# A recurrent layer's chunk chain: state and u in one tile, outputs directly behind their operands, v centred by a matmul, a third buffer of projection results

## The chip, the cores and the metric

The kernel runs on one core of one Trainium2 chip, as one launch. The metric is the device time of an execution in microseconds (us). The engines are named as the profile names them: PE is TensorE (PEld its weight loads), DVE is VectorE, ACT is ScalarE, POOL is GpSimd, and SP is the engine that here only issues DMAs; SPq is its queue.

## The reference

Two layers work on `x` of 1024 tokens and 1024 channels. The first is an RWKV-7 time-mixing layer, the second is differential attention with a gate; a norm ends it. The change lies in the first layer alone. Its core, per head of 64 channels, is a recurrence over the tokens and a group norm of its output:

```python
sa = einsum('bhij,bhj->bhi', state, a_t)
state = (state * w_t[:, :, None, :] + sa[..., None] * b_t[:, :, None, :]
         + v_t[..., None] * k_t[:, :, None, :])
y_t = einsum('bhij,bhj->bhi', state, r_t)
...
mean = jnp.mean(y, axis=-1, keepdims=True)
yn = (y - mean) * lax.rsqrt(var + GN_EPS)      # then * ln_w + ln_b, per head
o = (yn + bonus) * silu(g);  x = x + o @ w_out
```

r, k, v and g are projections of token-shifted mixtures of the normed input by 1024 x 1024 matrices. Since the recurrence is linear in v over the head's rows, and the mean of y is taken over the same rows, the kernel takes the mean of each head out of v before the recurrence, and y needs no centring behind it.

## The kernel before

All matrices are float32; the large projections are split in a high and a low part and done as three matmuls (L192, L193, L194 into `fl`). Layer 1 has three stages. Up to about 274 us the input is normed and turned, the low-rank paths run, and r, v and k of the first 512 tokens are projected. From 274 to 886 us the recurrence (the WKV stage) runs beside the rest of the projections and the output projection. From 914 us on matmuls of layer 2 stand beside what is left, and from 971 us they are alone.

The recurrence is cut into 16 groups. A group is 128 tokens (two chunks, c = 0 and 1, of 64 tokens) by 8 heads (four pairs). Five pieces of code (generators) handle a group, in slots; slot i runs chain of group i, norm of group i-1, merge of group i+1, prep of group i+3 and invert of group i+2, beside "fill", that is, steps of the projections and of the output projection (L285 to L287 and L291, with the residual `ev` loaded by L278).

- `prep` makes the scaled operands of a group (`ar`, `bk`, `pm`, `bkt`), and sends a small matrix through DRAM: L511 writes `dA`, L528 reads it back as `al`, spread over partitions.
- `invert` solves a triangular system in 31 steps on POOL; each step is one product (L551, tile `tm`) and one sum (L553, tile `xx`). Before it, DVE makes `ni` from `al` (L538 to L545), and POOL clears `xx` (L542). Its result leaves by L556 (`dX`) and comes back by L558 (`qd`). `xx` has two buffers, so the clearing for one group waits until the `dX` of the group two before has left its tile.
- `merge` completes the inverse (`q`), loads the centred v into the tile `uv` (L573), and copies v into a second tile `sv` (L608).
- `chain` goes through the two chunks in order: it puts the state into `sv` (L617), Z = matmuls of `sv` (L639), copies it (`zs`), U = matmuls by the inverse (L649), copied into `uv` (L651 by DVE, L652 by ACT), S = matmuls of `uv` (L658), `tn` = state + S (L661, DVE), the next state into `sv` (L665, DVE) and into the kept state `st` (L666, POOL). The chunk's output `y` is made by `out(c)`: eight matmuls from the state (L629) and eight from u and v (L632).
- `norm` copies `y` (L675) and does the group norm.

A projection step of v ends in `post` of `proj_step`: the result is copied to `ev` (pool `evp`), four transposes (L211) turn it, DVE sums each head (L215) and subtracts the mean (L217) into a second `ev` tile, and L220 sends that to `d_vc`.

The order of the instructions on each engine isn't the order of this code. The program is built under a scheduler that orders it from a model of durations and priorities (`PRI`), with the slots' tick counts as budgets; each engine then executes its list in order, and SP issues its DMAs in order too: a DMA that isn't ready holds those behind it in the list.

Of the kernel before, what the change touches and what calls it, by code (L numbers as in the profile page):

```python
# [11 lines left out]
F32 = mybir.dt.float32  # L12
# [3 lines left out]
ALU = mybir.AluOpType  # L16
AX = mybir.AxisListType
# [3 lines left out]
P = 128  # L21
# [3 lines left out]
C = 64  # L25
# [4 lines left out]
NU = 4  # L30
NC = 2
TM = NC * C
T = 13
# [43 lines left out]
class Trunk:  # L77
# [10 lines left out]
    def start(self, lp, xnT):  # L88

        nc, tc, I = self.nc, self.tc, self.I  # L90
        const = self.const
        self.ident = const.tile([P, P], F32, name="ident")
        make_identity(nc, self.ident)
        self.par = const.tile([P, len(ROWS), KT], F32, name="par")
        self.mug = const.tile([P, 6, KT], F32, name="mug")
        self.omg = const.tile([P, 6, KT], F32, name="omg")
        nc.gpsimd.memset(xnT[:, :, 0:1], 0.0)
        xts = []

        def load(tt):  # L100
            xts.append(lp.tile([P, KT, P], F32, name="xt", bufs=4).rearrange("p k t -> p (k t)"))
            nc.sync.dma_start(out=xts[tt], in_=I["x"][0, tt * P:(tt + 1) * P, :])
        for tt in range(4):
            load(tt)
        nc.sync.dma_start(out=self.par, in_=I["rows"])
        gb = self.par[:, COL["a_norm"]:COL["a_norm"] + 1, :].to_broadcast([P, 6, KT])
        nc.gpsimd.tensor_tensor(self.mug, self.par[:, 0:6, :], gb, op=ALU.mult)
        nc.gpsimd.tensor_tensor(self.omg, gb, self.mug, op=ALU.subtract)
        for t0 in range(0, KT, 2):
            ms = lp.tile([P, 2], F32, name="ms")  # L110
            for i in range(2):
                sq = lp.tile([P, D], F32, name="sq", bufs=1)
                nc.scalar.activation(sq, xts[t0 + i], AF.Square, accum_out=ms[:, i:i + 1])
            nc.vector.tensor_scalar(ms, ms, 1.0 / D, 1e-6, op0=ALU.mult, op1=ALU.add)
            rs = rsqrt(nc, lp, ms, [P, 2], "xr")
            for i in range(2):
                tt = t0 + i
                xs = lp.tile([P, KT, P], F32, name="xs").rearrange("p k t -> p (k t)")
                nc.vector.tensor_scalar_mul(xs, xts[tt], rs[:, i:i + 1])
                if tt + 4 < KT:  # L120
                    load(tt + 4)
                for hf in range(2):
                    pt = self.fps.tile([P, 4, P], F32, name="fl")
                    for q in range(4):
                        k = hf * 4 + q
                        nc.tensor.transpose(out=pt[:, q, :], in_=xs[:, k * P:(k + 1) * P], identity=self.ident)
                    dst = xnT[:, hf * 4:hf * 4 + 4, 1 + tt * P:1 + (tt + 1) * P]
                    if tt in (1, 3) or hf == 0 and tt > 3:
                        nc.vector.tensor_copy(out=dst, in_=pt)
                    else:  # L130
                        nc.scalar.copy(out=dst, in_=pt)
            yield
# [27 lines left out]
    def proj_step(self, hf, p, pr, src, group):  # L160

        nc, I = self.nc, self.I
        sl = slice(hf * TH, (hf + 1) * TH)
        G = {"w": []}
# [31 lines left out]
        def post(k):  # L196
            if k == 0:
                G["ev"] = ev = self.evp.tile([P, TH], F32, name="ev")
                if p == 3:
                    nc.scalar.activation(ev, G["ps"], AF.Sigmoid)  # L200
                    nc.vector.tensor_tensor(ev, ev, G["ps"], op=ALU.mult)
                else:
                    nc.scalar.copy(out=ev, in_=G["ps"])
                nc.sync.dma_start(out=self.d_in[p][pr, :, sl], in_=ev)
            if p != 2:
                return

            if k == 2:
                G["pt"] = pt = self.fps.tile([P, 4, P], F32, name="fl")
                for i in range(4):  # L210
                    nc.tensor.transpose(out=pt[:, i, :], in_=G["ev"][:, i * P:(i + 1) * P], identity=self.ident)  # L211
            if k == 4:
                ptv = G["pt"].rearrange("p i (h e) -> p (i h) e", e=64)
                mn = self.evp.tile([P, 8], F32, name="mn")
                nc.vector.tensor_reduce(mn, ptv, axis=AX.X, op=ALU.add)  # L215
                vc = self.evp.tile([P, 4, P], F32, name="ev")
                nc.vector.scalar_tensor_tensor(vc.rearrange("p i (h e) -> p (i h) e", e=64),  # L217
                                               mn.unsqueeze(2).to_broadcast([P, 8, 64]), -1.0 / 64, ptv,
                                               op0=ALU.mult, op1=ALU.add)
                nc.sync.dma_start(out=self.d_vc[sl, pr * P:(pr + 1) * P].rearrange("(i p) e -> p i e", p=P), in_=vc)  # L220
        return early, pre, mm, post, lambda: 650 if group["own"] is not G else 1300, 650

# [309 lines left out]
    def invert(self, M):  # L532

        nc, sb, sm = self.nc, self.sb, self.sm
# [12 lines left out]
        for s in range(31):  # L547
            n, w = s // 4 + 1, 31 - s
# [5 lines left out]
            yield 0  # L554
        dX = self.dr.tile([32, 8, 4, 32], F32, name="dX")
        nc.sync.dma_start(out=dX.rearrange("x k q t -> q x k t"), in_=xx)  # L556
        M["qd"] = qd = self.ub.tile([P, 8, 32], F32, name="qd", bufs=1)
        nc.sync.dma_start(out=qd, in_=dX.rearrange("(c x) k q t -> (x k q) c t", c=8))  # L558

    def merge(self, M):  # L560
# [3 lines left out]
        M["q"] = q = self.ub.tile([P, 8, C], F32, name="q")  # L564

        M["uv"] = uv = self.ub.tile([P, 2, 8, C], F32, name="uv")
        M["sv"] = sv = self.ub.tile([P, 2, 8, C], F32, name="sv")
        e0 = NU * M["j"] * P
        for h in range(2):
            for c in range(NC):  # L570
# [12 lines left out]
        for c in range(8):  # L583
            for h in range(2):
                o = h * 64
# [17 lines left out]
        for h in range(2):  # L603
            hs = slice(h * 64, h * 64 + 64)
            nc.scalar.copy(out=pm[hs, h, :, 0:64], in_=ar[hs, :, 0, :])
            yield 0
        for h in range(2):
            nc.scalar.copy(out=sv[64 - h * 64:P - h * 64, h], in_=uv[64 - h * 64:P - h * 64, h])  # L608

    def chain(self, M):  # L610

        nc, sm, ps = self.nc, self.sm, self.wps
        ar, pm, uv, sv, bkt, q, wc = (M[n] for n in ("ar", "pm", "uv", "sv", "bkt", "q", "wc"))
        HS = [slice(h * 64, h * 64 + 64) for h in range(2)]
        wt = self.state[M["j"]]
        for h in range(2):
            nc.scalar.copy(out=sv[HS[h], h, 0::NC, :], in_=wt[HS[h]])  # L617
        yield 1

        def out(c):  # L620
            if c == 0:
                M["y"] = ps.tile([P, 8, C], F32, name="y", bufs=1)
            y = M["y"]

            z = M["qt"] + c == 0
            pairs = [(u * NC + c, h) for u in range(NU) for h in range(2)]

            for uc, h in [] if z else pairs:
                nc.tensor.matmul(y[HS[h], uc, :], lhsT=sv[HS[h], h, uc, :], rhs=ar[HS[h], uc, 1, :], start=uc == c, stop=False,  # L629
                                 tile_position=(h * 64, h * 64))  # L630
            for uc, h in pairs:
                nc.tensor.matmul(y[HS[h], uc, :], lhsT=uv[:, h, uc, :], rhs=pm[:, h, uc, 64:P], start=z and uc == c,  # L632
                                 stop=uc == pairs[-1][0], tile_position=(0, h * 64))
        for c in range(NC):
            us = [(u, u * NC + c) for u in range(NU)]
            zp = ps.tile([P, NU, C], F32, name="zu", bufs=2)
            for u, uc in us:
                for h in range(2):
                    nc.tensor.matmul(zp[HS[h], u, :], lhsT=pm[:, h, uc, 0:64], rhs=sv[:, h, uc, :], start=True, stop=True,  # L639
                                     tile_position=(0, h * 64))  # L640
            zs = sm.tile([P, NU, C], F32, name="zs", bufs=1)
            nc.scalar.copy(out=zs, in_=zp)
            if c:
                out(c - 1)
            yield 1
            up = ps.tile([P, NU, C], F32, name="zu", bufs=2)
            for u, uc in us:
# [6 lines left out]
            if M["qt"] < S // TM - 1 or c < NC - 1:  # L654
# [7 lines left out]
                wb = wc[:, c::NC].unsqueeze(2).to_broadcast([P, NU, C])  # L662
                if c < NC - 1:
                    for h in range(2):
                        nc.vector.tensor_tensor(sv[HS[h], h, c + 1::NC, :], tn[HS[h]], wb[HS[h]], op=ALU.mult)  # L665
                nc.gpsimd.tensor_tensor(wt, tn, wb, op=ALU.mult)  # L666
            yield 1
        out(NC - 1)

    def norm(self, M):  # L670

        nc, sm, ps, nm = self.nc, self.sm, self.wps, self.nm
        j, t0 = M["j"], M["qt"] * TM
        y = nm.tile([P, NU, TM], F32, name="yt")
        nc.scalar.copy(out=y.rearrange("p u (c t) -> p (u c) t", t=C), in_=M["y"])  # L675
        y2 = nm.tile([P, NU, TM], F32, name="y2", bufs=1)
        nc.scalar.activation(y2, y, AF.Square)
        bv = nm.tile([P, NU, TM], F32, name="bv", bufs=1)
# [51 lines left out]
    def layer1(self):  # L730
# [9 lines left out]
        st = ExitStack()  # L740
        self.wp = st.enter_context(tc.tile_pool(name="wp", bufs=2, side="right", reuse_waits="tile"))
        self.xmp = st.enter_context(tc.tile_pool(name="xmp", bufs=XB, side="right", reuse_waits="tile"))
        self.evp = st.enter_context(tc.tile_pool(name="evp", bufs=2, side="right", reuse_waits="tile"))

        def src_of(hf):
            def src(k):
# [35 lines left out]
        for i in range(-3, 17):  # L782
# [1 line left out]
            if i == 13:  # L784
                fl = itertools.chain(fl, self.run(self.out_proj(512, 2, I["a_w_out"][0])))
            if 0 <= i < 16:
                st_.append((self.chain(Ms[i]), 8, 0, T))
            if 0 <= i - 1 < 16:
                st_.append((self.norm(Ms[i - 1]), 6, 0, T))
            if 0 <= i + 1 < 16:  # L790
                st_.append((self.merge(Ms[i + 1]), 9, 2, T))
            if 0 <= i + 3 < 16:
                st_.append((self.prep(Ms[i + 3], Ms[i + 4] if i < 12 else None), 12, 0, T))
            if 0 <= i + 2 < 16:
# [543 lines left out]
```

## Time and profile before

| what | value |
|---|---|
| device time, three runs | 1627.41, 1633.85, 1634.28 us; median 1633.85 us |
| profiled execution | 1635.44 us, its span 1633.6 us |
| PE busy in the span | 1494.4 us (91%) |
| DVE, ACT, POOL busy | 1194.8 us (73%), 909.6 us (56%), 672.8 us (41%) |
| mean granted clock of PE | 0.945 |

Busy time is the time in which an engine's instructions run. The span is cut below into stages, since the shares differ by stage. In a timeline a row has the start in us, the duration in us, the engine, the line of the kernel, what it writes and reads, and in brackets how long the engine sat idle before it and on what. The profile's granted clock is a share of TensorE's full 2.4 GHz; 0.5 is 1.2 GHz.

### The profile page before, as it was taken

To read this page: it belongs to the slowest core of one execution; us is meant where nothing else is said; L and a number is where in the kernel's file an instruction comes from. 1 tells how busy PE (TensorE), PEld (TensorE's weight loads), DVE (VectorE), ACT (ScalarE), POOL (GpSimd) and SP (SyncE) were. 2 spreads that over 40 slices of the span, in tenths; PEclk is the share of its full clock that TensorE was granted. 3 is DMA by queue.
4 is the path that set the end of the run, shared out by engine and by line. 5 is a ranking of instruction groups with operands and counts; after the bars stand their busy time and mean duration, and the time that the engine had idled before them with its cause. 6 is when DMAs were issued, how large, how long until landed. Compare 5 with 4: busy or idle time off the path is not lost.

```text
span 1633.6 us, 31095 instructions
## 1 busy us (share of the span) xinstructions
PE 1494.4 (91%) x10496; PEld 1208.3 (74%) x10496; DVE 1194.8 (73%) x3119; ACT 909.6 (56%) x2095; POOL 672.8 (41%) x1685
## 2 busy tenths in 40 slices
PE   3799999988998999979869789999999999999897
PEld 3577777666776777768758567788888888888786
DVE  7745658866879798788555777887878888787764
ACT  5645565745657586655234644665565656556420
POOL 4000003856878688778656111233232333333100
PEclk8799999989999999979879789999999999999999
DMA  7654677755656567656446451211111111113231
GB/s 195 187 185 144 186 226 216 201 163 152 194 157 175 164 179 190 185 160 174 128 142 164 131 169 58 67 46 31 46 46 27 46 33 40 40 40 119 92 126 52
DMA packets 218095, 207.39 MB, mean 127 GB/s; under 512 B 78032, under 2 KB 163280, under 8 KB 217936
## 3 DMA queue, kind: packets, MB, share of 16 engines
q1 hardware_dynamic: 217936, 205.40, 42.9%
q8 instruction: 83, 1.36, 0.3%
q14 instruction: 76, 0.62, 0.1%
HBM read 147.09 MB, written 58.27 MB: 126 GB/s over the span
## 4 chain that ended last, share of the span: by engine, by line
PE 63%; DVE 14%; DMA 7%; ACT 6%; issue 5%; POOL 4%; SPq 1%; ACTq 0%; DVEq 0%; POOLq 0%
PE pj L878 6%; PE pj L877 6%; PE pj L879 6%; PE fl L192 5%; PE fl L193 5%; PE fl L194 5%; PE tr L982 4%; PE sc L940 2%; PE sc L941 2%; PE tr L970 2%; POOL xx L553 2%; POOL tm L551 2%; DMA al<-dA 1%; PE sc L498 1%; PE tr L1255 1%
## 5 line engine op out<-in xcount | busy, mean ns | idle before, releaser
L192 PE MATMUL fl<-xh,wh 128*128 128x512 f32 x512 | 212.2, 420 | 11.2 <-DVE ev L217 8.8
L877 PE MATMUL pj<-wh,xh 128*128 128x512 f32 x512 | 214.1, 418 | 0.0
L193 PE MATMUL fl<-xl,wh 128*128 128x512 f32 x512 | 209.2, 410 | 3.7 <-DVE xl L151 3.7
L553 POOL TENSOR_TENSOR xx<-xx,tm 128x60 f32<-128x60 f32 (+24 forms) x496 | 196.8, 397 | 36.4 <-DVE xx L545 0.4
L194 PE MATMUL fl<-xh,wl 128*128 128x512 f32 x512 | 209.3, 410 | 0.0
L551 POOL TENSOR_TENSOR tm<-al,xx 128x60 f32<-128x60 f32 (+24 forms) x496 | 190.2, 383 | 40.4 <-DVE xx L545 4.0
L878 PE MATMUL pj<-wh,xl 128*128 128x512 f32 x512 | 202.7, 396 | 2.6 <-DVE xl L1216 2.6
L879 PE MATMUL pj<-wl,xh 128*128 128x512 f32 x512 | 202.1, 396 | 0.0
L157 DVE TENSOR_TENSOR wl<-wf,wh 128x512 fp32r<-128x512 f32 x160 | 119.0, 748 | 80.4 <-ACT wh L156 79.5
L946 ACT ACTIVATE p<-sc,mx 128x256 f32<-128x256 f32 (+7 forms) x128 | 94.6, 741 | 142.1 <-DVE mx L945 123.1
L926 POOL CAST kh<-kh 64x128 fp32r<-64x128 f32 x128 | 45.2, 353 | 263.4 <-ACT kh L918 250.0
L156 ACT CAST wh<-wf 128x512 fp32r<-128x512 f32 x160 | 97.6, 617 | 94.1 <-PE fl L193 71.6
L192 PEld LDWEIGHTS fl<-xh,wh 128*128 128x128 f32 x512 | 98.4, 192 | 40.3 <-issue 12.4
L193 PEld LDWEIGHTS fl<-xl,wh 128*128 128x128 f32 x512 | 99.0, 193 | 29.2 <-DVE xl L151 5.2
L194 PEld LDWEIGHTS fl<-xh,wl 128*128 128x128 f32 x512 | 98.7, 193 | 24.0 <-issue 1.4
L879 PEld LDWEIGHTS pj<-wl,xh 128*128 128x128 f32 x512 | 96.8, 189 | 21.9
L878 PEld LDWEIGHTS pj<-wh,xl 128*128 128x128 f32 x512 | 97.5, 190 | 19.6 <-DVE xl L1216 4.3
L877 PEld LDWEIGHTS pj<-wh,xh 128*128 128x128 f32 x512 | 97.5, 190 | 15.4 <-ACT xh L1215 0.2
L944 DVE TENSOR_REDUCE mx<-sc 128x1 f32<-128x256 f32 (+7 forms) x128 | 95.4, 753 | 0.8
L982 PEld LDWEIGHTS tr<-v,p 128*128 128x128 f32 x576 | 74.9, 194 | 7.8 <-ACT p L972 3.2
L982 PE MATMUL tr<-v,p 128*128 128x128 f32 x576 | 76.1, 278 | 2.1 <-ACT p L972 2.1
L940 PE MATMUL sc<-kh,q 128*128 128x512 f32 (+2 forms) x192 | 70.9, 378 | 4.0 <-issue 2.1
(295 smaller groups left out, 3695.3 us busy)
## 6 DMA issues: line engine op xcount, KB each, us to landing
wf<-in_a_w_in SPq DMA_DIRECT2D x64, 512.0 KB
d_in<-ev SPq DMA_DIRECT2D x64, 256.0 KB
wf<-in_b_w SPq DMA_DIRECT2D x64, 256.0 KB
xk<-d_xn SPq DMA_DIRECT2D x40, 256.5 KB
al<-dA SPq DMA_DIRECT2D x16, 512.0 KB
wf<-in_a_w_out SPq DMA_DIRECT2D x16, 512.0 KB
p<-d_x SPq DMA_DIRECT2D x10, 512.0 KB
d_c<-cc SPq DMA_DIRECT2D x16, 260.0 KB
```

The source lines that it names most:

```text
L156: self.nc.scalar.copy(out=wh, in_=wf)
L157: self.nc.vector.tensor_tensor(wl, wf, wh.bitcast(F32), op=ALU.subtract)
L192: nc.tensor.matmul(G["ps"], lhsT=wh[:, kk, :], rhs=xh, start=(k == 0), stop=False)
L193: nc.tensor.matmul(G["ps"], lhsT=wh[:, kk, :], rhs=xl, start=False, stop=False)
L194: nc.tensor.matmul(G["ps"], lhsT=wl[:, kk, :], rhs=xh, start=False, stop=(k == KT - 1))
L551: nc.gpsimd.tensor_tensor(tv, al[:, s:s + 1, s + 1:].to_broadcast([P, n, w]), xx[:, 0:n, s:s + 1].to_broadcast([P, n, w]), op=ALU.mult)
L553: nc.gpsimd.tensor_tensor(xx[:, 0:n, s + 1:], xx[:, 0:n, s + 1:], tv, op=ALU.add)
L877: nc.tensor.matmul(pf, lhsT=self.X[i][0][:, k], rhs=wh, start=(k == 0), stop=False)
L878: nc.tensor.matmul(pf, lhsT=self.X[i][1][:, k], rhs=wh, start=False, stop=False)
L879: nc.tensor.matmul(pf, lhsT=self.X[i][0][:, k], rhs=wl, start=False, stop=(k == KT - 1))
L940: nc.tensor.matmul(sc[:, b:e], lhsT=q[:, m], rhs=H["kh"][:, m, b:e], start=True, stop=False)
L982: nc.tensor.matmul(po, lhsT=at[:, b, :], rhs=H["v"][:, b, :], start=(b == 0), stop=(b == i))
```

## The change

- The tile `sv` goes. The rows of `uv` that will take u hold the state first: the state of a chunk is written there, Z and the state's part of the output read it, and then u is written over it. The copies of v (L608) go with it.
- A chunk's output from the state is emitted directly behind Z, and the one from u and v directly behind S and the state's update. `y` is copied at the end of the chain (to the tile `yt`), not at the beginning of the norm.
- v is turned by an ordinary matmul against `less` = identity minus the mean over each half of 64 rows, in place of a transpose; the reduction goes, and the subtraction becomes a copy. `less` is made once by POOL at the start (three clearings and one sum).
- The pool `evp` has three buffers where it had two; `qd` has two where it had one. The tick counts of `chain` and `merge` fall by one.

The core of the diff:

```diff
+        nc.gpsimd.tensor_tensor(self.less, self.less, self.ident, op=ALU.add)
...
-                    nc.tensor.transpose(out=pt[:, i, :], in_=G["ev"][:, i * P:(i + 1) * P], identity=self.ident)
+                    nc.tensor.matmul(pt[:, i, :], lhsT=G["ev"][:, i * P:(i + 1) * P], rhs=self.less, start=True, stop=True)
             if k == 4:
-                ptv = G["pt"].rearrange("p i (h e) -> p (i h) e", e=64)
-                mn = self.evp.tile([P, 8], F32, name="mn")
-                nc.vector.tensor_reduce(mn, ptv, axis=AX.X, op=ALU.add)
                 vc = self.evp.tile([P, 4, P], F32, name="ev")
-                nc.vector.scalar_tensor_tensor(vc.rearrange("p i (h e) -> p (i h) e", e=64),
-                                               mn.unsqueeze(2).to_broadcast([P, 8, 64]), -1.0 / 64, ptv,
-                                               op0=ALU.mult, op1=ALU.add)
+                nc.vector.tensor_copy(out=vc, in_=G["pt"])
...
-        M["qd"] = qd = self.ub.tile([P, 8, 32], F32, name="qd", bufs=1)
+        M["qd"] = qd = self.ub.tile([P, 8, 32], F32, name="qd", bufs=2)
...
-        M["sv"] = sv = self.ub.tile([P, 2, 8, C], F32, name="sv")
...
-        for h in range(2):
-            nc.scalar.copy(out=sv[64 - h * 64:P - h * 64, h], in_=uv[64 - h * 64:P - h * 64, h])
...
-            nc.scalar.copy(out=sv[HS[h], h, 0::NC, :], in_=wt[HS[h]])
+            nc.scalar.copy(out=uv[HS[h], h, 0::NC, :], in_=wt[HS[h]])
...
-            if c:
-                out(c - 1)
+
+            for uc, h in [] if z else pairs:
+                nc.tensor.matmul(y[HS[h], uc, :], lhsT=uv[HS[h], h, uc, :], rhs=ar[HS[h], uc, 1, :], start=uc == c, stop=False,
+                                 tile_position=(h * 64, h * 64))
...
-                        nc.vector.tensor_tensor(sv[HS[h], h, c + 1::NC, :], tn[HS[h]], wb[HS[h]], op=ALU.mult)
+                        nc.vector.tensor_tensor(uv[HS[h], h, c + 1::NC, :], tn[HS[h]], wb[HS[h]], op=ALU.mult)
                 nc.gpsimd.tensor_tensor(wt, tn, wb, op=ALU.mult)
+            for uc, h in pairs:
+                nc.tensor.matmul(y[HS[h], uc, :], lhsT=uv[:, h, uc, :], rhs=pm[:, h, uc, 64:P], start=z and uc == c,
+                                 stop=uc == pairs[-1][0], tile_position=(0, h * 64))
             yield 1
-        out(NC - 1)
+        M["yt"] = self.nm.tile([P, NU, TM], F32, name="yt")
+        nc.scalar.copy(out=M["yt"].rearrange("p u (c t) -> p (u c) t", t=C), in_=y)
...
-        self.evp = st.enter_context(tc.tile_pool(name="evp", bufs=2, side="right", reuse_waits="tile"))
+        self.evp = st.enter_context(tc.tile_pool(name="evp", bufs=3, side="right", reuse_waits="tile"))
...
-                st_.append((self.chain(Ms[i]), 8, 0, T))
+                st_.append((self.chain(Ms[i]), 7, 0, T))
...
-                st_.append((self.merge(Ms[i + 1]), 9, 2, T))
+                st_.append((self.merge(Ms[i + 1]), 8, 2, T))
```

How the scheduler's order changes is shown at three places. In the rows below a number behind a name tells one buffer from another, and "x8" counts equal instructions that follow each other.

On SP, around the end of the inversion of group 3 (at 433 us in the trace). Here `dX_4310` before and `dX_4278` after is the result of that inversion, `dA` and `al` are the matrix of group 5, and `qd` is the result coming back. Before:

```order
L556 DMA dX_4310<-xx_3768 4x256x32
L511 DMA dA_4346<-ab_4475 128x8x32
L700 DMA d_o_67<-yt_3711 128x4x128
L679 DMA bv_4344<-d_bv_2653 128x512
L204 DMA d_in1_61<-ev_4363 128x512
L204 DMA d_in1_61<-ev_4571 128x512
L441 DMA a_5437<-d_a_64 128x4x128
L558 DMA qd_4312<-dX_4310 128x8x32
L168 DMA wf_4798<-in_a_w_in 128x1024
L526 DMA d_bv_4844<-v_4285 128x512
L528 DMA al_4846<-dA_4346 128x1x1024
```

And after:

```order
L507 DMA dA_4310<-ab_4447 128x8x32
L741 DMA xk_5288<-d_xn0_69 128x513
L437 DMA a_5395<-d_a_64 128x4x128
L741 DMA xk_5329<-d_xn0_69 128x513
L169 DMA wf_4614<-in_a_w_in 128x1024
L524 DMA al_4807<-dA_4310 128x1x1024
L552 DMA dX_4278<-xx_3750 4x256x32
L522 DMA d_bv_4805<-v_4251 128x512
L688 DMA d_o_67<-yt_3662 128x4x128
L667 DMA bv_4308<-d_bv_2642 128x512
```

Before, the result `dX` stood ten places ahead of the load of `al`; now it stands directly behind that load. In the whole list such a neighbourhood (`al` directly ahead of `dX`) is found at four groups before, and after at the same four and this one.

On DVE, in the slot of the chain of group 3 (at 445 to 457 us in the trace), where `ni` is the first step of an inversion and `tn` the state's update. Before:

```order
L157 TENSOR_TENSOR wl<-wf,wh 128x512
L73 SCALAR_TENSOR_TENSOR gn_y<-gn_t,gn_y 128x8
L689 COPY y_4529<-gn_y 128x512
L538 TENSOR_SCALAR ni<-al 128x32
L539 RECIPROCAL ni<-ni 128x32
L540 TENSOR_TENSOR al<-al,ni 128x992
L545 COPY xx<-ni 32x8 x4
L661 TENSOR_TENSOR tn<-st_1998,zu 128x256
L590 COPY x_4581<-mg 32x256
L665 TENSOR_TENSOR sv<-tn,wc 64x4x64 x2
```

And after:

```order
L677 COPY y_4487<-gn_y 128x512
L646 TENSOR_TENSOR tn<-st_1987,zu 128x256
L650 TENSOR_TENSOR uv<-tn,wc 64x4x64 x2
L158 TENSOR_TENSOR wl<-wf,wh 128x512
L534 TENSOR_SCALAR ni<-al 128x32
L535 RECIPROCAL ni<-ni 128x32
L536 TENSOR_TENSOR al<-al,ni 128x992
L541 COPY xx<-ni 32x8 x4
L571 STREAM_TRANSPOSE x_4435<-qd 128x256
```

The state's update stood behind the four instructions that begin with `ni`; now it stands ahead of them.

On PE, the second output of one chunk and the first of the next, at one place of the stage (in the names, `y<-pm,uv` is the part from u and v, `y<-ar,sv` or `y<-ar,uv` the part from the state). Before:

```order
L658 MATMUL zu<-uv,bkt 64x64 x8
L632 MATMUL y<-pm,uv 64x64 x8
L518 MATMUL sc<-ident,bk 128x64
L522 MATMUL sc<-sq,bones 128x512
L586 MATMUL mg<-x_6167,pm 32x32 x16
L194 MATMUL fl<-xh,wl 128x512
L639 MATMUL zu<-sv,pm 64x64 x8
L629 MATMUL y<-ar,sv 64x64 x8
```

And after:

```order
L193 MATMUL fl<-xh,wh 128x512
L194 MATMUL fl<-xl,wh 128x512
L643 MATMUL zu<-uv,bkt 64x64
L653 MATMUL y<-pm,uv 64x64
L195 MATMUL fl<-xh,wl 128x512
L193 MATMUL fl<-xh,wh 128x512
L194 MATMUL fl<-xl,wh 128x512
L518 MATMUL sc<-sq,bones 128x512
L195 MATMUL fl<-xh,wl 128x512
L643 MATMUL zu<-uv,bkt 64x64 x7
L653 MATMUL y<-pm,uv 64x64 x7
```

Here the outputs stood directly behind S and directly behind Z before already; after, the first of them stands between the matmuls of S. Over all 32 chunks, in both lists, the first output from u and v comes one to eight matmuls behind the first of S, and the outputs from the state stand among or behind those of Z in 20 or more of 30 chunks, and elsewhere within 85 matmuls.

## Rows read from the trace of the kernel before

**Rows 1.** Windows by stage: stretch, length, busy time per engine, granted clock, DMA share

```profile
core 0 of [0], span 1633.6 us
core 0: us, PE busy (x) PEld busy (x) DVE busy (x) ACT busy (x) POOL busy (x), PEclk, DMA share, GB/s
...
274.00:886.00 612.00, 549.47 (x5563) 437.56 (x5561) 457.08 (x1031) 352.10 (x717) 454.79 (x1087) 0.92 0.61 171
787.00:797.00 10.00, 4.38 (x30) 3.81 (x31) 4.75 (x12) 2.35 (x6) 6.37 (x18) 0.52 0.61 172
```

**Rows 2.** POOL's costliest group, 274 to 886 us: busy, mean ns, idle before

```profile
L553 POOL TENSOR_TENSOR xx<-xx,tm 128x60 f32<-128x60 f32 (+24 forms) x495 | 196.6, 397 | 36.3 <-DVE xx L545 0.4
```

**Rows 3.** Waits of POOL, 274 to 886 us: total, times, longest us

```profile
POOL xx L542 <- DMA dX<-xx: 47.9, 10, 13.0
POOL st L666 <- DVE tn L661: 10.4, 5, 5.2
POOL bk L486 <- PE sc L518: 9.2, 3, 5.1
```

**Rows 4.** Timeline of SP's queue: start, us, engine, line, transfer

```profile
388.98 0.55 SPq L528 DMA_DIRECT2D al<-dA  x1
389.62 0.55 SPq L556 DMA_DIRECT2D dX<-xx  x1
390.36 8.91 SPq L220 DMA_DIRECT2D d_vc<-ev  x1
...
433.42 0.56 SPq L556 DMA_DIRECT2D dX<-xx  x1
...
439.26 0.68 SPq L558 DMA_DIRECT2D qd<-dX  x1
...
817.97 9.11 SPq L526 DMA_DIRECT2D d_bv<-v  x1
```

**Rows 5.** Timeline of POOL: start, us, instruction, idle before and its releaser

```profile
382.18 1.29 POOL L486 TENSOR_TENSOR bk<-m,em 128x512 f32<-128x512 f32 x1 [3.03 <-PE sc L518]
...
401.28 0.32 POOL L542 MEMSET xx<- 128x256 f32 x1 [8.75 <-DMA dX<-xx]
...
438.31 0.32 POOL L542 MEMSET xx<- 128x256 f32 x1 [1.27 <-DMA dX<-xx]
...
705.50 0.32 POOL L542 MEMSET xx<- 128x256 f32 x1 [3.80 <-DMA dX<-xx]
...
829.20 0.32 POOL L542 MEMSET xx<- 128x256 f32 x1 [12.97 <-DMA dX<-xx]
```

**Rows 6.** Timeline of DVE, then POOL, at 453 to 457 us

```profile
453.39 0.18 DVE L538 TENSOR_SCALAR ni<-al 128x32 f32<-128x32 f32 x1 [5.17 <-DMA al<-dA]
...
455.90 0.42 DVE L661 TENSOR_TENSOR tn<-st,zu 128x256 f32<-128x256 f32 x1
...
456.40 0.61 POOL L666 TENSOR_TENSOR st<-tn,wc 128x256 f32<-128x256 f32 x1 [5.24 <-DVE tn L661]
```

**Rows 7.** Timeline of PE at three idle times of the stage

```profile
368.10 0.76 PE L192 MATMUL fl<-xh,wh 128*128 128x512 f32 x1 [5.10 <-DVE ev L217]
...
792.62 0.58 PE L285 MATMUL fl<-wh,xh 128*128 128x256 f32 x1 [7.09 <-DVE ev L291]
...
831.68 0.44 PE L639 MATMUL zu<-sv,pm 128*64 128x64 f32 x2 [8.92 <-DVE sv L665]
```

**Rows 8.** Groups of instructions that the change removes or replaces, and L982 for comparison

```profile
L608 ACT COPY sv<-uv 64x512 f32<-64x512 f32 x32 | 19.7, 616 | 11.5 <-DMA uv<-d_vc 11.1
...
L215 DVE TENSOR_REDUCE mn<-fl 128x8 f32<-128x512 f32 x16 | 11.0, 689 | 11.0 <-PE fl L211 10.9
...
L217 DVE SCALAR_TENSOR_TENSOR ev<-mn,fl 128x512 f32<-128x512 f32 x16 | 10.9, 681 | 6.0 <-DMA d_vc<-ev 5.8
...
L982 PE MATMUL tr<-v,p 128*128 128x128 f32 x576 | 76.1, 278 | 2.1 <-ACT p L972 2.1
...
L211 PE MATMUL fl<-ident,ev 128*128 128x128 f32 x64 | 11.3, 298 | 0.5 <-ACT ev L203 0.5
```

More of the change, by code (lines that the diff above doesn't have):

```diff
@@ L606, in merge @@
             yield 0
-        for h in range(2):
-            nc.scalar.copy(out=sv[64 - h * 64:P - h * 64, h], in_=uv[64 - h * 64:P - h * 64, h])
     def chain(self, M):
         nc, sm, ps = self.nc, self.sm, self.wps
-        ar, pm, uv, sv, bkt, q, wc = (M[n] for n in ("ar", "pm", "uv", "sv", "bkt", "q", "wc"))
+        ar, pm, uv, bkt, q, wc = (M[n] for n in ("ar", "pm", "uv", "bkt", "q", "wc"))
         HS = [slice(h * 64, h * 64 + 64) for h in range(2)]
@@ L616, in chain @@
         for h in range(2):
-            nc.scalar.copy(out=sv[HS[h], h, 0::NC, :], in_=wt[HS[h]])
+            nc.scalar.copy(out=uv[HS[h], h, 0::NC, :], in_=wt[HS[h]])
         yield 1
[L620 to L633, printed above, removed]
+        M["y"] = y = ps.tile([P, 8, C], F32, name="y", bufs=1)
         for c in range(NC):
             us = [(u, u * NC + c) for u in range(NU)]
+            pairs = [(uc, h) for _, uc in us for h in range(2)]
+            z = M["qt"] + c == 0
             zp = ps.tile([P, NU, C], F32, name="zu", bufs=2)
@@ L638, in chain @@
                 for h in range(2):
-                    nc.tensor.matmul(zp[HS[h], u, :], lhsT=pm[:, h, uc, 0:64], rhs=sv[:, h, uc, :], start=True, stop=True,
+                    nc.tensor.matmul(zp[HS[h], u, :], lhsT=pm[:, h, uc, 0:64], rhs=uv[:, h, uc, :], start=True, stop=True,
                                      tile_position=(0, h * 64))
@@ L673, in norm @@
         j, t0 = M["j"], M["qt"] * TM
-        y = nm.tile([P, NU, TM], F32, name="yt")
-        nc.scalar.copy(out=y.rearrange("p u (c t) -> p (u c) t", t=C), in_=M["y"])
+        y = M["yt"]
         y2 = nm.tile([P, NU, TM], F32, name="y2", bufs=1)
@@ L742, in layer1 @@
         self.xmp = st.enter_context(tc.tile_pool(name="xmp", bufs=XB, side="right", reuse_waits="tile"))
-        self.evp = st.enter_context(tc.tile_pool(name="evp", bufs=2, side="right", reuse_waits="tile"))
+        self.evp = st.enter_context(tc.tile_pool(name="evp", bufs=3, side="right", reuse_waits="tile"))
+        self.less = self.evp.tile([P, P], F32, name="less", bufs=1)
+        nc.gpsimd.memset(self.less, 0.0)
+        for o in (0, 64):
+            nc.gpsimd.memset(self.less[o:o + 64, o:o + 64], -1.0 / 64)
         def src_of(hf):
```

## The prediction, made before the changed kernel was run

> **What bounds the kernel now.** I read the windows by stage first. The change touches only the stage of the recurrence, 274 to 886 us, and a few instructions before it. In that stage PE is busy for 549.47 of 612 us and POOL for 454.79 [rows 1]. PE is the fuller engine, but its list is mostly fill, which can move; so I went on to POOL's groups and its waits. One sum of an inversion step comes 495 times at 397 ns [rows 2], which is 16 inversions of 31 steps less one, and on POOL's timeline the inversions follow each other from 274 to 886 us without a pause. The operand of the next one is there well before it is needed. POOL is therefore a lane that paces the stage: the time not busy is made of its waits, the largest of which is the clearing of `xx` on the DMA that carries a result away, 47.9 us in ten waits; then the state on `tn`, 10.4, and `bk` on PE, 9.2 [rows 3]. The end of the last inversion sets the last chain and with it the tail.
>
> The clearings led me to SP's queue. Where `al` is issued directly ahead of `dX` (388.98 and 389.62), the issue of the DMA behind them takes 8.91 us, elsewhere 0.5 to 0.7; at the last of the four such places it is 9.11 [rows 4]. POOL's clearing, released when `dX` has landed, begins 11.7 us after that issue (389.62 to 401.28); it waits 8.75 and, at the last place, 12.97 us [rows 5]. Where `dX` stands alone (433.42), `qd`, which needs it, is issued at 439.26 with other DMAs between, and the clearing waited 1.27 [rows 5]. Last I read PE's own idle times: 5.10 us on the centred v, 7.09 on a residual tile, 8.92 on the next state [rows 7].
>
> **The change, part by part.** All sums are made against the profiled execution, 1635.4 us; the median of the three runs is 1.6 lower, and the forecast is given on the median.
>
> The copies of v: 32 x 616 ns = 19.7 us of ACT go [rows 8]. ACT is busy 352 of 612 us [rows 1], and none of POOL's large waits names it, so I cost this at 0; if chain steps did wait for ACT there it would give back up to the 19.7. Since u overwrites the state, its copies must follow the outputs that read the state. Those stand beside Z, ahead of U, in PE's list of before too, and U waits for a copy of Z anyway: 0, at most the length of eight small matmuls per chunk. The outputs directly behind their operands: the order of before has them there already, so 0 both ways. The copy of y only changes its place on ACT: 0.
>
> The centring: 16 reductions, 11.0 us of DVE, go, and 16 subtractions of 681 ns become copies of the same tile [rows 8]. DVE is busy 457 of 612 us, so this matters only where PE or SP waits for that result; that is the 5.10 us stall below. The 64 turning matmuls replace 64 that take 298 ns [rows 8]. The trace has no such matmul against a mean matrix; the nearest row is an ordinary float32 matmul of the same 128 x 128 shape, 278 ns [rows 8]. Bounds: -64 x 0.02 = -1.3 us by that row and, by the longest matmul among the rows, 0.76 us for four times the columns [rows 7], 64 x 0.46 = +30 us; I take 0, since the row of the same shape is the nearer.
>
> The Trainium skill, page "TensorE: Matmul & The Clock Gate", section "Terms", says that the transpose mode is four times as fast for FP32; by it 64 ordinary matmuls would cost three more such durations each, 64 x 3 x 0.298 = 57 us at most of PE (an estimate). By that rule this edit alone could make the kernel slower; the trace doesn't bear it out, with 298 ns for the transpose and 278 ns for the matmul.
>
> Making `less`: four POOL instructions at the start, where POOL waits long for parameters: 0, or some 1 us if that cover were gone.
>
> The third `evp` buffer: the stalls of 5.10 (the second `ev` tile had to wait for a DMA that frees its buffer, then PE for DVE) and of 7.09 (a residual not loaded early enough) should go [rows 7]. They lie on PE, not on POOL's lane. Only what POOL waits for PE passes on: the `bk` of 382.18 waited 3.03 us [rows 5] for PE matmuls that the 5.10 us stall had made late. I take -3.0; the bounds are 0 and the two stalls, -12.2.
>
> The order of DVE: the state's update stands ahead of `ni` now. Before, `ni` waited 5.17 us for `al`, the update behind it came at 455.90, and POOL stood 5.24 us for it [rows 6]. That goes: -5.2 (bounds 0 and -5.2). `ni` comes later by the update's three instructions, and isn't waited for at once.
>
> The clearings' places on POOL: by the order, the clearing moves two to four inversion steps later in three groups (the 3.80 us wait of 705.50 and the 12.97 of 829.20 are two of them [rows 5], at four steps each) and two earlier in two that do wait or may. A step is two instructions of some 0.4 us [rows 2], so -1.6 - 3.2 - 3.2 + 1.6 + 1.6 = -4.8. Bounds 0, if a wait only moves along, and -8.0 without the two that lose.
>
> The order of SP: `dX` of group 3 now stands directly behind `al` of group 5, a fifth such pair. That `al` can only go when the inversion is over and its matrix is written. The trace prices such a pair at a clearing that waits 8.75 or 12.97 us where this one waited 1.27 [rows 5]. The clearing here also moves from the 5th to the 11th step, 6 x 0.8 = 4.8 us later. So the wait grows by between 12.97 - 1.27 = +11.7 and 8.75 - 4.8 - 1.27 = +2.7. I take +9, nearer the upper row, since `dX` can be held by `al` too.
>
> Sum: -3.0 - 5.2 - 4.8 + 9 = -4.0 us on POOL's lane. Forecast: 1633.85 - 4.0, about 1630. With all gains and the lower end of the last term, -13.0 + 2.7 = -10.3; without the clearings' gain and with its upper end, -8.2 + 11.7 = +3.5: own range 1624 to 1637.
>
> **Rivals.**
>
> PE sets the stage, not POOL. For it: PE is 90% busy there, POOL 74%. Against it: the fill can move while inversions can't. Then the stalls of 5.10 and 7.09 count in full, and the half clock around the second (0.52 in 787 to 797 us [rows 1]) gives 10 x 0.48 = 4.8 us: -17.0. POOL would have to follow: beyond the sum, its waits for the state (10.4 less 5.2) and for `bk` (9.2 less 3.0) can give 11.4 more, -15.4 in all. I price it at -15, 1619 us.
>
> The fifth pair decides. Place: SP's queue behind `dX` of group 3. If `dX` is held by its `al` and lands as late as at 829 us, the clearing waits 12.97, +11.7, and the lane is shifted by that. The gains upstream of it don't count if the update and `bk` find their operands late again behind the delayed d_vc and weight loads. 1633.85 + 11.7 = 1646 us. It decides from a wait of 1.3 + 13.0 = 14.3 us if all the gains hold, and from 1.3 if none does.
>
> The change doesn't do what it says: the outputs stand where they stood, the removed copies were idle time, the gains and losses on the lane cancel: 1634 us.
>
> The matmuls in place of the transposes are the slow ones: with the upper bound of that part, +30 us, of which PE's idle tenth hides a third or so, 20 us stay on the path: 1654 us. With 298 and 278 ns in the trace I give it little. (The rule of the Trainium skill's page "TensorE: Matmul & The Clock Gate" in "Terms" would put it there.)
>
> **How the numbers follow.** Forecast 0.45; PE 0.25; fifth pair 0.20; nothing 0.08; slow matmuls 0.02. A difference of 0.5%, 8 us, is about what a measurement of this kernel can tell from no change. Below 1625.7 lie nearly all of the PE case (0.24) and the low end of the forecast (0.12): faster 0.36. Above 1642 lie nearly all of the fifth pair (0.19) and the slow matmuls: slower 0.21. The rest, 0.43, is the same. The range must take in the PE case with its full 17 us and more, as well as the fifth pair: 1612 to 1647.
>
> **What would show it.** Each term has its place in the profile after: the `bk` wait near 382 us gone; no wait of the state on `tn` near 456; the wait of the clearing on `dX` in sum near 47.9 + 9 - 4 = 53 us in eleven waits or so, with a slow issue on SP behind a fifth pair near 434; the 5.10 and 7.09 us stalls of PE gone, but the inversions still back to back and the last ending near 883. The forecast is wrong if the last inversion ends more than 8 us from 886, or if the inversions show gaps where they wait for `ni`, which would mean that POOL isn't the lane; or if layer 2, whose code is the same, changes its length.

## The result, and the profile after

The changed kernel takes 1650.11 us (median of four runs, 1647.14 to 1652.07) where the kernel before takes 1632.68 (four runs); the ratio is 1.0111, 95% interval 1.0083 to 1.0139. It is slower, by 17 us, and lies above the predicted range. In the later comparisons the kernel before had medians of 1635.0 to 1636.8 over 11 to 19 runs, so the loss is better called 13 to 17 us. Times below are medians, and ratios are to the kernel before on the same chip. The changed kernel was timed in this comparison alone: where a gain below is a difference from 1650.1, the ratios would make it 2 to 6 us larger.

The profiled execution has a span of 1648.5 us. The stage of the recurrence by windows, in the same stretch as [rows 1]:

```profile
core 0: us, PE busy (x) PEld busy (x) DVE busy (x) ACT busy (x) POOL busy (x), PEclk, DMA share, GB/s
274.00:886.00 612.00, 551.70 (x5425) 439.83 (x5423) 447.33 (x1002) 331.66 (x680) 438.01 (x1058) 0.90 0.60 165
```

ACT and DVE are less busy, as forecast (331.66 for 352.10, 447.33 for 457.08). PE ran 138 matmul instructions fewer in this window, and POOL was busy 17 us less because it waited more and so got less far. POOL's waits, from 274 to 898 us, where the last inversion now ends (12 us later than before):

```profile
POOL xx L538 <- DMA dX<-xx: 45.6, 10, 9.3
POOL st L651 <- DVE tn L646: 19.7, 8, 4.6
POOL m L474 <- ACT m L460: 17.1, 6, 7.3
POOL bk L482 <- PE sc L514: 11.8, 4, 4.8
```

The wait on dX is about what it was [rows 3]; the waits on other engines, which were to shrink, have grown: the state on `tn` from 10.4 to 19.7, `bk` from 9.2 to 11.8, `m` from 7.7 to 17.1. Group by group, the ends of the inversions keep within 4 us of before until 588 us, where they are 3 us ahead. Then they fall behind: 4.8 us at 632, 10.4 at 671, 4.3 at 703, 14.2 at 752 and 20.7 at 796 us. The last groups give 8.6 of that back. DVE's waits on one load, `xm`, in the kernel before and in the changed one:

```profile
DVE xm L259 <- DMA xm<-d_o: 13.0, 5, 8.2
```

```profile
DVE xm L255 <- DMA xm<-d_o: 19.3, 5, 7.4
```

The two longest of the changed kernel fall into this stretch. The timeline of SP's queue, then DVE, PE and POOL around them:

```profile
607.41 0.56 SPq L524 DMA_DIRECT2D al<-dA  x1
...
612.79 0.32 SPq L252 DMA_DIRECT2D xm<-d_o  x1
...
684.82 0.55 SPq L524 DMA_DIRECT2D al<-dA  x1
...
687.16 0.34 SPq L252 DMA_DIRECT2D xm<-d_o  x1
```

```profile
617.40 0.41 DVE L636 COPY uv<-zu 64x256 f32<-64x256 f32 x1
625.17 0.69 DVE L255 TENSOR_TENSOR xm<-xm,xk 128x512 f32<-128x512 f32 x1 [7.36 <-DMA xm<-d_o]
...
696.84 0.69 DVE L255 TENSOR_TENSOR xm<-xm,xk 128x512 f32<-128x512 f32 x1 [7.18 <-DMA xm<-d_o]
697.44 0.41 DVE L636 COPY uv<-zu 64x256 f32<-64x256 f32 x1
```

```profile
626.51 0.80 PE L193 MATMUL fl<-xh,wh 128*128 128x512 f32 x1 [7.61 <-DVE ev L202]
...
632.06 0.62 PE L643 MATMUL zu<-uv,bkt 128*64 128x64 f32 x13
...
697.91 1.41 PE L643 MATMUL zu<-uv,bkt 128*64 128x64 f32 x15 [6.60 <-DVE uv L636]
```

```profile
445.73 0.32 POOL L538 MEMSET xx<- 128x256 f32 x1 [6.86 <-DMA dX<-xx]
...
629.31 1.28 POOL L474 TENSOR_TENSOR m<-kk,m 128x512 f32<-128x512 f32 x1 [7.30 <-ACT m L460]
```

A load `xm` of the output projection is issued 2.3 to 5.4 us behind an `al`, and DVE's product that needs it starts 9.7 to 12.4 us after the issue. DVE takes its instructions in order, but the two stalls do different harm.

At 617 us the chain's copy of u (617.40) stands ahead of the product; what stands behind it is `ev` (L202) and `sq` (L502). PE's fill waits 7.61 us for `ev`, and in PE's list 14 of the chain's 16 matmuls S stand behind that fill: they run from 632.06 on, 14.7 us after DVE's copy of u. ACT waits 6.90 us for `sq`, and POOL's `m` 7.30 us for ACT. Two windows of this stretch, with the columns as above:

```profile
621.00:624.50 3.50, 0.00 (x0) 0.00 (x0) 0.00 (x0) 0.00 (x0) 0.78 (x4) 0.56 0.26 92
626.00:632.00 6.00, 5.49 (x13) 4.12 (x13) 6.00 (x18) 3.95 (x7) 2.45 (x5) 0.53 0.74 231
```

For 3.5 us nothing runs but a little of POOL, with a quarter of the 16 DMA engines busy. Behind the stall, after PE's 7.61 idle us, the granted clock is 0.53, near the lower of its two levels (1.2 GHz). The fill ahead of S is slower too: its matmuls start every 0.43 us, where they started every 0.23 at 614 us.

At 690 us the copy of u itself (697.44) stands behind the product, and PE waits 6.60 us for it. POOL goes on with its inversion there; its waits on `tn` and `bk`, 2.2 to 4.6 us each, come from 705 us on. How much of these is the stall's is taken up below (e13).

The kernel before had such a stall of DVE once, late: 8.22 us at 831 us, behind which PE waited the 8.92 us of [rows 7].

The turning matmul, the other surprise, by lines:

```profile
L212 PE MATMUL fl<-less,ev 128*128 128x128 f32 x128 | 20.3, 300 | 0.5 <-ACT ev L204 0.5
```

64 matmuls are 128 PE instructions, where 64 transposes were 64 [rows 8].

### The profile page after: what moved, and what is told of

It reads as the page before. It is cut to its first block, busy times and chain, and to the rows that moved or that the text cites. A ratio compares the mean times of both kernels' runs of the same rounds, so it can differ in the third digit from the quotient of the medians.

```text
span 1648.5 us, 31133 instructions
## 1 busy us (share of the span) xinstructions
PE 1512.1 (92%) x10560; PEld 1226.1 (74%) x10560; DVE 1190.7 (72%) x3103; ACT 894.0 (54%) x2065; POOL 667.1 (40%) x1689
## 4 chain that ended last, share of the span: by engine, by line
PE 60%; DVE 13%; DMA 11%; ACT 5%; POOL 5%; issue 4%; SPq 1%; DVEq 0%; ACTq 0%; POOLq 0%
PE pj L872 6%; PE pj L870 6%; PE pj L871 6%; PE fl L193 5%; PE fl L194 5%; PE fl L195 5%; PE tr L975 4%; DMA dX<-xx 2%; PE sc L933 2%; POOL tm L547 2%; POOL xx L549 2%; DMA xm<-d_o 2%; PE sc L934 2%; PE tr L963 2%; PE sc L494 1%
## 5 line engine op out<-in xcount | busy, mean ns | idle before, releaser
L547 POOL TENSOR_TENSOR tm<-al,xx 128x60 f32<-128x60 f32 (+24 forms) x496 | 184.0, 371 | 42.3 <-DVE xx L541 4.6
L158 DVE TENSOR_TENSOR wl<-wf,wh 128x512 fp32r<-128x512 f32 x160 | 113.6, 716 | 90.7 <-ACT wh L157 90.1
```

The lines of the kernel that those rows point to most:

```text
L158: self.nc.vector.tensor_tensor(wl, wf, wh.bitcast(F32), op=ALU.subtract)
L547: nc.gpsimd.tensor_tensor(tv, al[:, s:s + 1, s + 1:].to_broadcast([P, n, w]), xx[:, 0:n, s:s + 1].to_broadcast([P, n, w]), op=ALU.mult)
```

## Experiments

Two theories at first. A: the one DMA that spreads `al` holds a part of the DMA engines for 7 to 9 us; what is issued behind it (`dX`, `xm`, others), in its shadow, lands late, and the new order puts more of what is waited for there. B: the chain itself became longer.

**al in four DMAs (e1 on the changed kernel, e2 on the kernel before).**

```diff
-nc.sync.dma_start(out=al, in_=dA.rearrange(...).unsqueeze(0).to_broadcast([4, 32, 1024]))
+for k in range(4):
+    nc.sync.dma_start(out=al[32 * k:32 * k + 32], in_=dA.rearrange(...))
```

> The changed kernel, but al is loaded by four DMAs of 32 partitions each instead of one broadcasting DMA. Theory A (the one broadcasting DMA keeps a few DMA engines for 7 to 9 us, what is issued behind it lands late, and in the changed kernel two operand loads xm of the output projection fall there, at 607 and 685 us, and stop DVE in its order for 7.4 and 7.2 us, the chain's u copies behind them): the two stalls of DVE go, and with them POOL's waits of 6 to 9 us on dX; the time falls from 1650 to 1610-1632. Theory B (the chain itself is longer, since u now overwrites the state): the DMA's form only takes out the waits on dX, both kernels gain alike, the changed one stays 12 to 20 us above the kernel before with the same edit.

> The kernel before with al in four DMAs. Theory A: its DVE stall of 8.2 us near 830 us and POOL's waits on dX (8.0, 8.8, 9.1, 13.0 us) go; 1600-1625 us, within 8 us of the changed kernel with the same edit. Theory B: 12 to 20 us below the changed kernel with the same edit. If a single DMA's width isn't what delays the others, both stay within 5 us of their times without the edit.

Measured: 1606.97 us (0.9833, 0.9793 to 0.9873) and 1612.51 us (0.9865, 0.9844 to 0.9887). Both gain, the changed kernel 43 us (from 1650.1) and the kernel before 23 (from 1635.3 beside it), and the changed one is no longer the slower. B falls. But the scheduler gave both a new order.

**Parts of the change undone (e3, e4) or alone (e10).** e3: `evp` with two buffers. e4: transposes, DVE's reduction and subtraction as before. e10: on the kernel before, only the chain's part, `qd` and the tick counts.

> The changed kernel with two evp buffers as before. By the order, dX stands directly behind al at four groups instead of five, and two of the loads xm still stand close behind an al. Theory A: one wait of 7 to 9 us less, 1636-1650 us. Theory B: the buffer has nothing to do with it, 1645-1655 us. Theory C (the third buffer helps as it was priced on PE): slower than the changed kernel by 5 to 17 us, 1655-1667 us.

> The changed kernel, but v is turned by transposes and centred by DVE's reduction and subtraction as before. Theory A: five groups have dX directly behind al as in the changed kernel, and the loads xm stand behind al at three groups, so 1640-1658 us, whatever the turning costs. Theory D (the matmuls in place of the transposes are slow, 20 us or more): 1625-1635 us.

> The kernel before with the part of the change that concerns the chain alone (state and u in one tile, the outputs' places, the copy of y, qd's second buffer, the tick counts); the turning of v and the two evp buffers as before. If the chain's part costs by itself (theory B): 1645-1655 us, the whole loss. If the loss is the turning matmul and the place of loads behind al: 1630-1642 us; the order has five groups with dX directly behind al.

Measured: e3 1643.01 us (1.0052, 1.0035 to 1.0069), e4 1636.96 us (1.0006, 0.9989 to 1.0024), e10 1638.41 us (1.0016, 1.0000 to 1.0033). The chain's part is worth nothing, as forecast, with or without the third buffer; the loss appears when the turning matmul is added. e4 came out below what theory A alone expected, so the matmul or the order that it brings matters.

**The matmul's price (e5; e17 with the order kept).**

```diff
-nc.tensor.matmul(pt[:, i, :], lhsT=G["ev"][...], rhs=self.less, start=True, stop=True)
+nc.tensor.transpose(out=pt[:, i, :], in_=G["ev"][...], identity=self.ident)
```

v stays uncentred in both. In e17 the scheduler is told that the transpose costs what the matmul did, and every engine's order stays that of the changed kernel.

> The changed kernel with the matmul against less replaced by a plain transpose, and v left uncentred (the mean isn't taken out at all), everything else as changed. It prices the matmul itself: 64 transposes are 64 PE instructions, 64 such matmuls stand as 128 instructions of 300 ns in the trace. Theory D (the turning matmul is what costs): at least the 9 us of PE come back, and more where they lay on the path, 1630-1641 us, and the first inversion ends 4 to 5 us earlier. Theory A alone: the order keeps dX behind al at four groups, and two loads xm stay behind an al; 1640-1650 us, the gain only from stalls that moved.

> The changed kernel with its order kept on every engine, the matmul against less replaced by a plain transpose and the mean of v left in: the price of the matmul alone, 128 PE instructions against 64. If PE's 9 us lie on the path: 5 to 10 us less, 1640-1645 us. If other work hides them: 1647-1652 us.

Measured: e5 1644.67 us (1.0053, 1.0035 to 1.0071), e17 1642.40 us (1.0027, 1.0001 to 1.0053). In e5, whose order is its own, DVE waits only 3.9 us for `xm`, and yet it lies above the kernel before; where it loses isn't worked out. e17, by the line's own view:

```profile
L212 PE MATMUL fl<-ident,ev x64: 270/273/474, 151.2 to 404.4; 128*128 128x128 f32 x64
```

Half the instructions at the same duration, and some 8 us less by the medians, 14 by the ratios. In e17's timeline the first inversion ends at 302.6 us, in the changed kernel's at 310.2, and the last 8.4 us earlier: the difference is there almost whole by 310 us, behind the first half of v. PE's time on L212 accounts for only 3.7 us of it there (8.53 against 4.85 us), and in e13, e15 and e16 below, which keep the matmul, the first inversion ends at 306.9 to 309.3. So the price in time is uncertain by several us.

**xm asked for early (e6), and with al in four DMAs (e8).** The loads of `xm` and `xk` are issued two steps ahead of the product, with two more buffers for `xm`.

> The changed kernel, with the operands xm of the output projection asked for two steps before DVE multiplies them (four buffers instead of two). Up to about 600 us the order is that of the changed kernel. Theory A: DVE's stalls of 7.4 and 7.2 us on xm go, and PE's of 7.6 and 6.6 us with them; 1630-1642 us, unless the additional group with dX directly behind al (group 13) takes 7 us back. Theory B or D: these stalls hide nothing, 1645-1655 us.

> The changed kernel with xm asked for early and al in four DMAs. Theory A: with al out of the way the loads xm are no longer late, so asking early brings little: 1600-1610 us. If the loads xm are late for another reason than al, it brings as much as it does without al's edit, 8 us or more: below 1600 us.

Measured: e6 1655.25 us (1.0128, 1.0078 to 1.0178), e8 1611.39 us (0.9838, 0.9798 to 0.9877). e6 is a miss for theory A as I had put it. DVE's timeline of e6:

```profile
612.80 0.69 DVE L264 TENSOR_TENSOR xo<-xo,xk 128x512 f32<-128x512 f32 x1 [5.83 <-DMA xk<-d_in]
```

The product now waits for its other operand, which had come to stand behind an `al`; three `dX` late in the stage stand there too, where the changed kernel had two. Here the load moved out of the shadow left its place to another. With `al` in four DMAs asking early brings nothing (e8 beside e1's 1606.97).

**A third buffer of xx (e9, and e11 and e12 with al in four DMAs).**

```diff
-xx = sb.tile([P, 8, 32], F32, name="xx")
+xx = sb.tile([P, 8, 32], F32, name="xx", bufs=3)
```

> The changed kernel with a third buffer of xx, so that POOL's clearing needn't wait until the last result has been carried away; up to about 800 us every engine's order is that of the changed kernel, and al is one DMA as there. Premise of the prediction (POOL's lane of inversions paces the stage): POOL's 45.6 us of waits on dX go, the inversions move up, 1612-1635 us. Theory A in its narrow form (what al delays stops DVE in its order, and that is the loss): POOL's waits only turn into others, DVE's stalls on xm stay, 1640-1652 us.

> The changed kernel with al in four DMAs and a third buffer of xx. Premise of the prediction: the 16.5 us that POOL still waits on dX there go too, 1592-1602 us. Theory A: with al out of the way little is left to gain, 1602-1610 us.

Measured: e9 1644.23 us (1.0053, 1.0033 to 1.0073), e11 1606.26 us (0.9826, 0.9780 to 0.9872). e9 doesn't test the premise, and e11 doesn't either: there POOL still waits 15.2 us on `dX`. The waits of POOL in e9:

```profile
POOL xx L538 <- DMA dX<-xx: 42.2, 9, 8.9
```

The scheduler used the free buffer to clear one group earlier, at the same place in POOL's list, where the clearing waits for the same `dX`.

> The changed kernel with transposes and DVE's centring as before, and al in four DMAs. If the matmul's 9 us of PE count on the path there too: 1597-1603 us, 5 to 9 us below the changed kernel with al in four DMAs (1607). If only the order made the difference of the two: 1604-1612 us.

> The same two edits on the changed kernel with v turned by transposes and centred by DVE as before. If the turning matmul's 9 us of PE count once POOL waits less: 5 to 9 us below the kernel with the matmul and the same two edits; if not, within 4 us of it.

> The changed kernel with v turned by transposes and centred by DVE as before, al in four DMAs, the order that of the kernel with the transposes and the broadcasting DMA. Without al's shadow all versions should come out alike, 1600-1608 us, the matmul's 9 us making the difference to the changed kernel with its order and the same DMAs (1606) if they lie on the path.

With transposes and DVE's centring: e7 1609.17 us (0.9832, 0.9791 to 0.9873), e12 1604.16 us (0.9809, 0.9775 to 0.9844), e18, which keeps e4's order, 1614.13 us (0.9848, 0.9826 to 0.9869). None is clearly below its partner with the matmul, and e18 lies above e13 (1605.85, next part), against what I expected: without the shadow the matmul's price can't be seen, and why isn't settled.

**al's shadow with every engine's order kept (e13 to e16).** The scheduler is told that the four DMAs cost what the one did; the lists of all engines are then those of the kernel that is edited, but for `al` itself. In e15 and e16 only some groups have the four DMAs.

> The changed kernel with al in four DMAs as in the first experiment, but every engine's list of instructions is that of the changed kernel, word for word (the scheduler is told that the four cost what the one did). Theory A: the gain of the first experiment comes from al's shadow itself, so most of it is there with the order kept: 1610-1630 us. Rival: the first experiment's gain was a luckier order; with the order kept 1640-1650 us.

> The kernel before with al in four DMAs and its own order kept on every engine. Theory A: 1608-1625 us, and the distance of the changed kernel to it, 17 us with the broadcasting DMA, shrinks to 8 us or less. Rival (the changed order costs in itself): both gain alike and the distance stays at 12 to 20 us.

> The changed kernel with its order kept, and al in four DMAs only for groups 9 to 13, behind which the loads xm and others that DVE and ACT wait for stand; the five groups with dX directly behind al keep the broadcasting DMA. If the loss is in these loads (the stalls at 617 and 690 us and what follows): 1630-1640 us. If it is in POOL's waits on dX: 1644-1650 us.

> The changed kernel with its order kept, and al in four DMAs only for groups 3, 4, 5, 14 and 15, behind which dX stands directly. Premise of the prediction (POOL's lane paces the stage, and its waits on dX are lost time): 20 to 30 us less, 1620-1630 us. If POOL's lane has slack: 1638-1650 us.

Measured: e13 1605.85 us (0.9816, 0.9787 to 0.9846), e14 1603.59 us (0.9809, 0.9784 to 0.9833), e15 1635.24 us (0.9988, 0.9964 to 1.0011), e16 1628.20 us (0.9953, 0.9937 to 0.9968). In an unchanged order the shadow costs the changed kernel 44 us (from 1650.1) and the kernel before 33 (from 1636.8 in the same comparison); without it 2 us lie between them, which can't be told from nothing. The last inversion moves by as much: from 898.7 to 854.7 us and from 886.6 to 853.0.

Set beside e13, the changed kernel's inversions take 12.8 us longer from 586 to 671 us and 2.0 from there to 752; beside e15, 9.3 and 5.3. So of the two nearly equal stalls of DVE the first, which holds S behind the fill, is the dear one: in e13 the rest of S runs 4.9 us after DVE's copy of u. POOL's waits in e13:

```profile
POOL bk L482 <- PE sc L514: 11.1, 5, 4.9
POOL st L652 <- DVE tn L647: 8.4, 7, 3.8
POOL m L474 <- ACT m L460: 4.5, 4, 2.1
```

Those on `tn` and `m` shrink with the shadow gone, the one on `bk` hardly. Waits of e15, then of e16:

```profile
POOL xx L542 <- DMA dX<-xx: 49.7, 10, 9.0
...
DVE xm L255 <- DMA xm<-d_o: 3.8, 4, 1.7
```

```profile
POOL xx L542 <- DMA dX<-xx: 23.9, 11, 3.7
...
DVE xm L255 <- DMA xm<-d_o: 19.9, 6, 6.8
```

e15 takes the loads out of the shadow (19.3 to 3.8 us of DVE's waits on `xm`) and gives 15 us; e16 takes `dX` out of it (45.6 to 23.9 us of POOL's waits) and gives 22. The two add up to 37 of the 44. Both ways of losing are real, and POOL's waits count about one for one.

How the DMA differs shows where `al` stands directly ahead of `dX`. SP's queue in the changed kernel, then at the same place in e13:

```profile
796.11 0.56 SPq L524 DMA_DIRECT2D al<-dA  x1
796.76 0.56 SPq L552 DMA_DIRECT2D dX<-xx  x1
797.37 9.59 SPq L437 DMA_DIRECT2D v<-d_in  x1
```

```profile
760.42 1.71 SPq L525 DMA_DIRECT2D al<-dA  x4
762.23 0.56 SPq L553 DMA_DIRECT2D dX<-xx  x1
762.83 2.80 SPq L437 DMA_DIRECT2D v<-d_in  x1
```

In the trace's packet records `al` is 128 packets of 4096 bytes. As one DMA they run 3.4 to 4.0 at a time in the last five groups and the last ends 8.4 to 10.9 us behind the issue; as four, 9 to 12 at a time, and it ends 3.7 to 6.1 us behind the first issue (e13). The Trainium skill, page "DMA: Bandwidth & Descriptors", section "Rules for kernel authors", says that an outermost dimension smaller than 16, such as a leading broadcast of c copies, confines a DMA to at most c engines; here c is 4, and the trace agrees with 3.4 to 4.0.

Beside e14 (1603.59), e13 and e12 (1605.85 and 1604.16) beat both kernels: the edit of `al` is worth 33 us to the kernel before, and the change adds nothing to it.

## Why the prediction was wrong, by its steps

- Right: the places. ACT's removed copies gave nothing by themselves; the outputs stood where they stood (e10: 1.0016); the 5.10 and 7.09 us stalls of PE went; `bk` at 384 us waits 0.67 us instead of 3.03; the state at 456 us no longer waits for `ni`.
- Right in kind: POOL's lane of inversions paces the stage, and its waits on `dX` are lost time (e16: 22 us of waits, 22 us of time). In all 20 traces the span goes on for 746 to 752 us behind the end of the last inversion, which lies anywhere from 852.6 to 898.7.
- Right within their bounds: the fifth pair and the clearings. The clearing at 445.73 waits 6.86 us, +5.6 where I took +9 between 2.7 and 11.7; with the 5.24 us gone the inversion lasts what it did, 37.5 us for 37.8. Without that pair the waits on `dX` fell by 7.9 us, where I took 4.8.
- **Wrong, the step that failed: "The order of SP".** I read the slow issue behind `al` as a matter of `dX` alone and counted pairs. The same rows showed that `d_vc` and `d_bv` were held too (8.91 and 9.11 us [rows 4]). I should have gone through the list for what stands within ten places behind every `al` and asked which engine waits for it in its order. Two loads `xm` had come there; the stalls of 7.36 and 7.18 us that they make were in no term and in no rival. The rival of the fifth pair had the mechanism and nearly the time, 1646 us, but at the wrong place: at 434 us nothing was lost on balance. That its time came near is luck.
- Wrong with it: I let POOL's waits on other engines shrink; they grew by about 20 us, `tn` and `m` above all. In this way DVE's stalls reach POOL's lane (in e13 the two fall from 36.8 to 12.9 us).
- **Mis-sized: the turning matmul,** taken at 0, measured at 9.0 us of PE (20.3 for 11.3) and about 8 us of time (e17, uncertain by several us). I took line L982's 278 ns as the duration of a matmul; its 576 instructions are 288 matmuls of two instructions each (by the code, 36 for each of 8 heads). The Trainium skill's rule on the transpose mode ("TensorE: Matmul & The Clock Gate", "Terms"), which I set aside on that ground, had the right sign: the measured factor is about two, not four: there are twice the instructions, each of 275 ns (median), where a transpose takes 273.

What isn't settled: how the 13 to 17 us divide. The shadow costs the changed order some 11 us more than the old one and the matmul about 8, which is 2 to 6 us more than the loss, so a little of the hoped-for gain may be in it; no run measures that alone.

## What to carry to other kernels

When a change moves a schedule, list what is issued behind each slow transfer, before and after, and which engine waits for it in order: here that was worth more than all removed work. A load that many partitions share is worth trying in parts whose outermost dimension is wide: here four parts of 32 partitions. A wait of an engine off the critical path may cost more than its length, through what stands behind it in another engine's list. Ask how many instructions one matmul makes before taking a row's mean as its price: a float32 matmul of 128 x 128 stood as two.

## What the runs showed of the hardware that I had not expected

- One broadcasting DMA of 512 KB used about 4 of the 16 DMA engines, and it was not done for 8.4 to 10.9 us; loads issued up to 5.4 us behind it were waited for until 9.7 to 12.4 us after their issue. The same bytes in four DMAs, with the order kept, gave 33 us of 1637 and 44 of 1650.
- Two stalls of DVE of nearly the same length, 7.36 and 7.18 us, stood among inversions that took 9 to 13 us and 2 to 5 us longer than in e15 and e13.
- A buffer more needn't remove a wait: with a third `xx` the clearing moved one group ahead and waited 42.2 us for the same transfers.
